# A hybrid Fourier / gated-delta step: the projection stream and its head chains issued in program order, placed by a build-time account of engine times

## The chip, the cores and the metric

The kernel runs on one core of a Trainium2 chip. The metric is the device time of one execution in microseconds (us), median of the runs shown; lower is better. A core has a matrix engine (PE in the profile, which lists its weight loads apart as PEld), a vector engine (DVE), a scalar engine (ACT), a general one (POOL) and a queue that only issues DMAs (SP). Each engine works through its own queue in order; between engines, semaphores say when an operand is ready.

## The reference

One layer with 128 context and 512 latent tokens of width 2048. After an RMS norm and a modulation, one input projection (2048 to 7216 columns) gives a Fourier group, twelve heads of q, k, v and a gate z, and per head and direction a decay and a beta. The heads run a gated delta rule in chunks:

```python
a = lmat + eye
t_inv = triangular_solve(a, eye, left_side=True, lower=True)
...
def step(s, inp):
    u_i, w_i, a_i, qg_i, kd_i, gl_i = inp
    v_new = u_i - einsum(w_i, s)
    o_i = einsum(qg_i, s) + einsum(a_i, v_new)
    s = s * exp(gl_i) + einsum(kd_i, v_new)
    return s, o_i
```

It is run forwards and backwards over the tokens, and the two results are added, normalised and multiplied with silu(z). The Fourier group is a 2D or 3D transform per channel group. All is joined (2048), goes through one output projection, and is added to the input with a gate; a last RMS norm follows. Outputs are both token streams and the final context states of all heads.

## The kernel before

Everything is float32. The three large products are split in two parts (hi and lo, float32r) and computed as three products; the small ones stay float32, which PE runs as two passes (two records in the trace).

**Start.** x is transposed and normalised, the modulation is computed from w_mod, and the first tiles of the projection (k, v, q of head 0, the decays, u of three Fourier groups) are computed while it goes on.

**The projection stream** (`stream`, L1015). Fifty tiles of 128 columns follow, in the order k1 q1 v1 z0 u3, then k, v, q of head h and z of head h-1, and at last f0 to f3 and z11. A tile is two halves of 320 tokens with 48 matmuls each, 4800 in all. Its weights come in on ACT's DMA queue (`raw`, two buffers) and are split by ACT (`whi`, L136) and POOL (`wlo`, L137), five buffers each. Three PSUM banks (`mbank`) take the tiles, five (`bank`) everything else.

**The chains beside it** are Python generators:

- a convolution with SiLU for each k, v, q tile (`conv`, L540 to L554), and the gate z (`after_z`), written to DRAM;
- `solve(h)`: transposes of k, the Gram product (L624), then the inverse of the 32 x 32 triangular blocks on DVE, a series of multiply (L670) and reduce (L672) pairs on 40 partitions; it goes out to DRAM and back twice (`NP`, `DD`);
- `delta(h)`: first the preparation, that is transposes of v, the decays E (L726), the block products that make the full inverse T (L740, L753, L768, L775) and the sums of q squared (`jq`, L786); then the scan, five steps for both directions at once. A step is KT x S (L805), r on DVE (L808), QT x S (L812), T x r (L823), vn on ACT (L826), kd x vn (L831), S on DVE (L839), AT x vn (L844) and the update of o on DVE. It ends with the normalisation of o;
- `head_out(h)`: transposes of o, times z, to DRAM; `fourier(f)`; and `res_gates`, which computes the gates of the residual.

A k or q tile of head i may be evacuated only when `delta(i - 2)` is done (`needs`), since KT and QT have two buffers.

**The output projection** (`out_stream`, L1208) takes the results back from DRAM (`load_y`) in the order heads 0 to 10, Fourier 0 to 3, head 11, in four column passes, 960 matmuls.

What sets the order: the main loop at the file's end runs the stream step by step and resumes each generator when a written-out latency has passed (`yield 3.00, 0.9` means 3 us of waiting and 0.9 us of PE work). That gives the program order. The framework's scheduler then takes it as a priority only: whenever an instruction of an engine isn't ready in its own reckoning, it takes a later one that is. So a stream matmul of a later tile can be issued ahead of a scan step that was written before it.

Of the kernel before, what the change touches and what calls it, by code (L numbers as in the profile page):

```python
# [69 lines left out]

@with_exitstack
def hybrid_step(ctx: ExitStack, tc: tile.TileContext, x_prompt, x_sample, state_ctx, c, c_ctx,
# [3 lines left out]
    PE, ACT, DVE, POOL, SP = nc.tensor, nc.scalar, nc.vector, nc.gpsimd, nc.sync  # L76
    w_mod, w_in, w_out = w_mod[0], w_in[0], w_out[0]
# [366 lines left out]
    def early_back(i, dst, at):  # L444
        SP.dma_start(out=dst[:, at:at + P], in_=ed[i][:, 0:P])
        SP.dma_start(out=dst[:, at + P + (at > 0):at + NT + (at > 0)], in_=ed[i][:, P:NT])
        n, c = (P, i - 1) if i else (48, 3)
        for m, a, b in ((1, at, at + P), (0, at + P + (at > 0), at + NT + (at > 0))):
            ACT.activation(dst[0:n, a:b], dst[0:n, a:b], AF.Identity, bias=ebias[0:n, c, m:m + 1])
# [12 lines left out]
    g = gp.enter_context(tc.tile_pool(name="gdn", bufs=1))  # L462
    def gates():
        abT = g.tile([P, NT], F32, tag="pj", name="abT", bufs=2)
        early_back(0, abT, 0)
        yield 1.50, 0
        pb = bank()
        for t in range(5):
            PE.matmul(pb[:, 48 * t:48 * t + 48], lhsT=abT[:, P * t:P * (t + 1)], rhs=K("sel_ab"), start=True, stop=True)
        pbv = pb[:, 0:240].rearrange("p (t c) -> p c t", c=48)  # L470
        yield 3.00, 0.3
# [20 lines left out]
        yield 5.00, 0.6  # L492
# [8 lines left out]
        yield 0.00, 0  # L501
        gT = g.tile([24, NT], F32, tag="KT", name="gT", bufs=2)
# [5 lines left out]
        yield 4.50, 1.1  # L508
        SP.dma_start(out=gd, in_=gT)
        gT2 = g.tile([24, 4, 5, 32], F32, tag="QT", name="gT2", bufs=2)  # L510
# [27 lines left out]
    def conv(col, parts, dst):  # L538
        ct = (col - C_Q) // P
# [4 lines left out]
        if isinstance(parts, int):  # L544
            early_back(parts, pj, 1)
# [3 lines left out]
        th = g.tile([P, 641], F32, tag="th", name="th", bufs=1)  # L549
        ACT.mul(dst, pj[:, 0:641], cw[:, ct:ct + 1])  # L550
        DVE.scalar_tensor_tensor(dst, pj[:, 1:642], cw[:, 36 + ct:37 + ct], dst, ALU.mult, ALU.add)
        DVE.scalar_tensor_tensor(dst, pj[:, 2:643], cw[:, 72 + ct:73 + ct], dst, ALU.mult, ALU.add)
        ACT.activation(th, dst, AF.Tanh)
        DVE.scalar_tensor_tensor(dst, th, 1.0, dst, ALU.add, ALU.mult)  # L554

# [11 lines left out]
    def after_k(h, parts):  # L567
        s = st_h[h]
        s["KT"] = g.tile([P, 641], F32, tag="KT", name="KT", bufs=2)
        conv(C_K + P * h, parts, s["KT"])  # L570

    def after_v(h, parts):
        s = st_h[h]
        s["vT"] = g.tile([P, 641], F32, tag="vT", name="vT", bufs=1)
        conv(C_V + P * h, parts, s["vT"])

    def after_q(h, parts):
        s = st_h[h]
        s["QT"] = QT = g.tile([P, 641], F32, tag="QT", name="QT", bufs=2)
        conv(C_Q + P * h, parts, QT)  # L580


    def after_z(k, parts):
        zs = g.tile([P, NT], F32, tag="zs", name="zs", bufs=2)
        for a, b, p in parts:
            ACT.activation(zs[:, a:b], p, AF.Tanh, scale=0.5)
            DVE.scalar_tensor_tensor(zs[:, a:b], zs[:, a:b], 1.0, p, ALU.add, ALU.mult)
        SP.dma_start(out=yd[k], in_=zs)

# [6 lines left out]
    def solve(h):  # L596
# [8 lines left out]
        yield 1.50, 0.6  # L605
# [22 lines left out]
        yield 4.50, 1.1  # L628
# [7 lines left out]
        yield 2.50, 0  # L636
# [4 lines left out]
        yield 3.50, 0  # L641
# [6 lines left out]
        yield 6.00, 0  # L648
# [6 lines left out]
        for i in range(1, 8):  # L655
# [5 lines left out]
            yield 1.20, 0  # L661
# [12 lines left out]
        for q in (0, 16):  # L674
            prod(YB[:, 0:8, 0:8], N2[:, q + 8:q + 16, q:q + 8], X2[:, q:q + 8, q:q + 8])
            prod(X2[:, q + 8:q + 16, q:q + 8], X2[:, q + 8:q + 16, q + 8:q + 16], YB[:, 0:8, 0:8])
            yield 2.00, 0
        for r0 in (0, 8):
            prod(YB[:, r0:r0 + 8, 0:8], N2[:, 16 + r0:24 + r0, 0:16], X2[:, 0:16, 0:8])
            yield 3.00, 0  # L680
        prod(YB[:, 0:16, 8:16], N2[:, 16:32, 8:16], X2[:, 8:16, 8:16])
        yield 3.00, 0
        prod(X2[:, 16:24, 0:16], X2[:, 16:24, 16:24], YB[:, 0:8, :])
        yield 3.00, 0
        for c0 in (0, 8):
            prod(X2[:, 24:32, c0:c0 + 8], X2[:, 24:32, 16:32], YB[:, :, c0:c0 + 8])
            yield 3.00, 0
        xd = dram.tile([40, 32, 32], F32, tag="xd", name="xd", bufs=2)
        SP.dma_start(out=xd, in_=X2)
        for b in range(4):  # L690
            SP.dma_start(out=DD[32 * b:32 * b + 32, 0:2].rearrange("p d t c -> p (d t) c"),
                         in_=xd[10 * b:10 * b + 10].rearrange("u r c -> r u c"))
        yield 6.00, 0
        f2 = "p d t c -> p (d t c)"
        DVE.transpose(DD[:, 2:4].rearrange(f2), DD[:, 0:2].rearrange(f2))
        yield 2.00, 0
# [585 lines left out]
```

## Time and profile before

| | us |
|---|---|
| median of 3 runs | 1534.41 (1528.46 to 1538.11) |
| the profiled execution, its own time | 1528.22 |
| its span, first to last instruction | 1526.2 |
| stream: first and last matmul start | 184.6 and 1266.7 |
| output projection: its first matmul starts | 1269.9 |
| mean granted PE clock | 0.975 of full speed |

In the rows of the profile, `mbank<-h_hi,whi` is an instruction that writes `mbank` and reads `h_hi` and `whi`; L and a number is the kernel's line; x and a number counts records. In the groups the columns are busy time, mean time of one in ns, and the idle time before them with what ended it. In the timeline they are start, length, engine, and in brackets the idle time before, with what ended it. A window's row is the stretch, its length, the busy time of PE, PEld, DVE, ACT and POOL, the granted clock, the share of the DMA engines and GB/s. Half clock shows as 0.5 in single stretches; the number of a window is a mean.

### The profile page before, as it was taken

To read this page: it belongs to the slowest core of one execution; us is meant where nothing else is said; L and a number is where in the kernel's file an instruction comes from. 1 tells how busy PE (TensorE), PEld (TensorE's weight loads), DVE (VectorE), ACT (ScalarE), POOL (GpSimd) and SP (SyncE) were. 2 spreads that over 40 slices of the span, in tenths; PEclk is the share of its full clock that TensorE was granted. 3 is DMA by queue.
4 is the path that set the end of the run, shared out by engine and by line. 5 is a ranking of instruction groups with operands and counts; after the bars stand their busy time and mean duration, and the time that the engine had idled before them with its cause. 6 is when DMAs were issued, how large, how long until landed. Compare 5 with 4: busy or idle time off the path is not lost. (4 is left out here: it accounts for less than half of the span.)

```text
span 1526.2 us, 27377 instructions
## 1 busy us (share of the span) xinstructions
PE 1407.7 (92%) x10548; PEld 1270.9 (83%) x10548; DVE 882.6 (58%) x1594; ACT 635.1 (42%) x1678; POOL 643.5 (42%) x759
## 2 busy tenths in 40 slices
PE   6999989889989998989999898999999999999996
PEld 5676989788878897978999898888988998888885
DVE  4455257586867677394756748394856534422025
ACT  5343375244262543526254353526353244322234
POOL 2223346425252542434364344444363433236575
PEclk9999999899999999999999999999999999999999
DMA  9899434315253544433223223323233336386103
GB/s 309 294 336 318 149 114 124 86 39 148 89 157 104 153 119 121 136 96 84 76 84 82 77 80 89 91 72 85 77 95 96 104 114 193 120 301 193 56 1 138
DMA packets 251664, 198.35 MB, mean 130 GB/s; under 512 B 43465, under 2 KB 221590, under 8 KB 251406
## 3 DMA queue, kind: packets, MB, share of 16 engines
q1 hardware_dynamic: 130926, 124.77, 25.5%
q10 hardware_dynamic: 120608, 71.84, 16.5%
q8 instruction: 83, 1.36, 0.4%
q14 instruction: 47, 0.39, 0.1%
HBM read 172.57 MB, written 23.99 MB: 129 GB/s over the span
## 5 line engine op out<-in xcount | busy, mean ns | idle before, releaser
L137 POOL TENSOR_TENSOR wlo<-raw,whi 128x512 fp32r<-128x512 f32 (+1 forms) x276 | 382.1, 1389 | 583.1 <-ACT whi L136 481.1
L1015 PE MATMUL mbank<-h_hi,whi 128*128 128x320 f32 x1600 | 522.9, 327 | 0.0
L1015 PE MATMUL mbank<-h_hi,wlo 128*128 128x320 f32 x1600 | 506.9, 317 | 4.3 <-POOL wlo L137 4.2
L1015 PE MATMUL mbank<-h_lo,whi 128*128 128x320 f32 x1600 | 506.8, 317 | 0.0
L1015 PEld LDWEIGHTS mbank<-h_hi,whi 128*128 128x128 f32 x1600 | 309.8, 194 | 10.5 <-issue 7.9
L1015 PEld LDWEIGHTS mbank<-h_hi,wlo 128*128 128x128 f32 x1600 | 308.6, 193 | 7.3 <-POOL wlo L137 5.6
L1015 PEld LDWEIGHTS mbank<-h_lo,whi 128*128 128x128 f32 x1600 | 309.8, 194 | 1.9 <-issue 1.6
L136 ACT CAST whi<-raw 128x512 fp32r<-128x512 f32 (+1 forms) x276 | 168.2, 614 | 241.1 <-PE mbank L1015 60.8
L670 DVE TENSOR_TENSOR tmp<-NP,XB 40x1024 f32<-40x1024 f32 (+1 forms) x60 | 109.9, 1832 | 1.3
L670 DVE TENSOR_TENSOR tmp<-XB,YB 40x1024 f32<-40x1024 f32 (+1 forms) x60 | 105.8, 1763 | 1.0
L818 POOL TENSOR_SCALAR kd<-k,edl 128x128 f32<-128x128 f32 x96 | 59.8, 634 | 41.6 <-PE bank L831 41.4
L548 ACT COPY pj<-mbank 128x128 f32<-128x128 f32 (+2 forms) x99 | 30.0, 339 | 87.5 <-PE mbank L1015 68.1
L1208 PE MATMUL mbank<-wlo,y_hi 128*128 128x512 f32 x160 | 62.8, 393 | 2.8 <-POOL wlo L137 2.0
L805 PE MATMUL bank<-S,KT 128*128 128x128 f32 x192 | 36.5, 301 | 30.4 <-DVE S L839 30.4
L1208 PE MATMUL mbank<-whi,y_hi 128*128 128x512 f32 x160 | 63.8, 399 | 0.0
L726 ACT ACTIVATE E<-gb,ngg 128x128 f32<-128x128 f32 x120 | 42.2, 394 | 51.8 <-DVE AT L728 31.6
L1208 PE MATMUL mbank<-whi,y_lo 128*128 128x512 f32 x160 | 62.4, 390 | 0.0
L1208 PE MATMUL bank<-whi,y_lo 128*128 128x512 f32 x160 | 62.3, 389 | 0.0
L1208 PE MATMUL bank<-whi,y_hi 128*128 128x512 f32 x160 | 62.3, 389 | 0.0
L1208 PE MATMUL bank<-wlo,y_hi 128*128 128x512 f32 x160 | 62.2, 389 | 0.0
L672 DVE TENSOR_REDUCE YB<-tmp 40x64 f32<-40x512 f32 (+2 forms) x60 | 59.7, 995 | 1.4
L672 DVE TENSOR_REDUCE XB<-tmp 40x64 f32<-40x512 f32 (+2 forms) x60 | 59.7, 995 | 1.3
(319 smaller groups left out, 2440.8 us busy)
## 6 DMA issues: line engine op xcount, KB each, us to landing
raw<-in_w_in ACTq DMA_DIRECT2D x104, 512.0 KB
wm<-in_w_mod SPq DMA_DIRECT2D x64, 512.0 KB
gw<-in_w_mod SPq DMA_DIRECT2D x32, 512.0 KB
raw<-in_w_out ACTq DMA_DIRECT2D x48, 256.0 KB
gb<-gd SPq DMA_DIRECT2D x12, 640.0 KB
yd<-zs SPq DMA_DIRECT2D x16, 320.0 KB
zl<-yd SPq DMA_DIRECT2D x16, 320.0 KB
yd<-zl SPq DMA_DIRECT2D x16, 320.0 KB
```

What stands on the lines that cost most here:

```text
L136: ACT.copy(whi, raw_part)
L137: sub.tensor_tensor(wlo, raw_part, whi, ALU.subtract)
L548: ACT.copy(pj[:, a:b], ps)
L670: DVE.tensor_tensor(tv, A.unsqueeze(2).broadcast_to(s4), B.rearrange("p j c -> p c j").unsqueeze(1).broadcast_to(s4), ALU.mult)
L672: DVE.tensor_reduce(dst, tv, AX.X, ALU.add)
L726: ACT.activation(E[:, 1 - d], gb[:, d, P * t:P * (t + 1)], AF.Exp, bias=ngg4[:, d, h, t:t + 1])
L805: PE.matmul(pks[:, P * d:P * (d + 1)], lhsT=KT[:, a:a + P], rhs=S[:, d], start=True, stop=True)
L818: POOL.tensor_scalar(kd[:, d], k[:, tt[d], :], edl4[:, d, h, tt[d]:tt[d] + 1], 1.0, ALU.mult, ALU.mult)
L1015: PE.matmul(pm[:, 0:320], lhsT=w, rhs=h[k][:, a:b], start=n == 0, stop=n == 3 * NK - 1)
L1208: PE.matmul(acc[t], lhsT=a[kk][:, sl], rhs=w, start=kk == order[0] and j == 0, stop=kk == order[-1] and j == 2)
```

## The change

The latencies at the `yield`s go. In their place stands `Estimate`, called for every instruction as it is built. It keeps a time for each engine and each tile, prices an instruction by its engine, shape and operands (a float32r matmul at 13.5 ns + n / 2.4 ns, a two-operand DVE instruction on 40 partitions at 0.15 us + n / 960 x 1.75 us, and so on), and starts it when its engine, its operands and its buffer are free by that account. A generator is resumed when all that it issued last is done by the account and PE's time is past it by `GUARD`, 0.2 us. Where the stream can't go on, PE's time is set forward to the next such point.

Around the whole main loop stands `tc.manual_schedule()`: from the stream on, the framework takes the program order as it is.

Other edits: `delta` is cut into `prep` and `scan`, run by generators of their own, so that the preparation of the next head may go on beside a scan; `conv` and `after_z` become generators; `take` and `room` count the buffers of `pj`, `th` and `zs`; `th` and `v` get a second buffer; `gT` and `gT2` use the slots of `o` and `v`; the loads of `DD` wait until the head before has read it; the Fourier groups wait for `delta` of head 10.

```diff
+class Estimate:
...
+    def __call__(self, inst, *_):
...
+        t = self.free[engine]
+        for x in ins:
+            y = self.of(x.tensor)
+            t = max(t, y[0] + (0.1 if y[1] != engine else 0.0))
...
+            end = t + self.cost(op, engine, inst, outs, ins)
+            self.free[engine] = end
...
+    room = {"pj": 2, "th": 2, "zs": 2}
...
+    def conv(kind, h, parts):
+        yield from take("pj")
...
-    def delta(h):
+    def prep(h):
...
-        s["v"] = v = g.tile([P, 5, P], F32, tag="v", name="v", bufs=1)
+        s["v"] = v = g.tile([P, 5, P], F32, tag="v", name="v", bufs=2)
...
-        yield 2.50, 1.1
-
-        jq = g.tile([P, 641], F32, tag="th", name="jq", bufs=1)
+        yield
+        yield from take("th")
+        jq = g.tile([P, 641], F32, tag="th", name="jq", bufs=2)
...
+    def scan(h):
...
         while h and ("out", h - 1) not in done:
-            yield 5.50, 0
+            yield "poll"
...
-                yield 3.00, 0.9
+                yield
...
-            while not all(x in done or x[1] < 0 for x in needs(kind, i)):
+            while not (all(x in done or x[1] < 0 for x in needs(kind, i)) and room["pj" if kind in "kqv" else "zs"]):
                 yield
...
-            while not {("u", f), ("f", f), "E_last"} <= done:
-                yield 8.00, 0
+            while not {("u", f), ("f", f), "E_last", ("delta", NH - 2)} <= done:
+                yield "poll"
...
+    def advance():
+        moved = True
+        while moved:
+            moved = False
+            for x in list(live):
+                while x in live and (x[2] is None or x[2] + GUARD <= est.free["PE"]):
+                    poll = x[2] is None
+                    resume(x)
+                    if poll and x[2] is None:
+                        break
+                    moved = True
...
+    ordered = tc.manual_schedule()
+    ordered.__enter__()
...
     while running or live:
+        t = est.free["PE"]
         if running:
             running = next(main, "end") != "end"
-            clock += 0.82
         else:
             next(tail)
-            clock += 3.25
...
+        if est.free["PE"] == t:
+            waits = [x[2] for x in live if x[2] is not None]
+            est.free["PE"] = max(t + 0.05, min(waits) + GUARD if waits else t + 0.5)
+        advance()
```

The lines of the changed kernel are about 150 further down: the stream is L1163, KT x S L948, r L951, QT x S L955, T x r L966, vn L969, kd x vn L974, S L982, AT x vn L987, the solve's pairs L804 and L806, the output projection L1384.

What the change moves shows in the queues. PE's queue in the second and third step of the scan of head 0, before (`h_hi` and `h_lo` are the parts of the stream's input, `whi` and `wlo` of its weights; the numbers are those of buffers):

```order
L831 MATMUL bank_3357<-vn_3322,kd_3318 128x128 x2
L844 MATMUL bank_3363<-vn_3322,AT_2799 128x128 x2
L1015 MATMUL mbank_3508<-h_hi_406,wlo_3297 128x320
L805 MATMUL bank_3372<-S_3360,KT_2079 128x128
L812 MATMUL bank_3373<-S_3360,QT_2109 128x128
L1015 MATMUL mbank_3508<-h_hi_407,whi_3314 128x320
L1015 MATMUL mbank_3508<-h_lo_423,whi_3314 128x320
L1015 MATMUL mbank_3508<-h_hi_407,wlo_3315 128x320
L823 MATMUL bank_3386<-r_3374,KK_2396 128x128 x2
L1015 MATMUL mbank_3508<-h_hi_408,whi_3314 128x320
```

The same place in PE's queue now:

```order
L974 MATMUL bank_3363<-vn_3358,kd_3354 128x128 x2
L987 MATMUL bank_3369<-vn_3358,AT_2802 128x128 x2
L948 MATMUL bank_3378<-S_3366,KT_2119 128x128 x2
L955 MATMUL bank_3379<-S_3366,QT_2221 128x128 x2
L966 MATMUL bank_3396<-r_3380,KK_2495 128x128 x2
L974 MATMUL bank_3402<-vn_3397,kd_3393 128x128 x2
L987 MATMUL bank_3408<-vn_3397,AT_2802 128x128 x2
L948 MATMUL bank_3415<-S_3405,KT_2119 128x128 x2
```

The stream's matmuls have left the scan; heads 1 to 9 read the same, where before 24 of them stood between the steps of most heads, and the next stream matmul of the changed queue comes after the scan. DVE's queue in the scan of head 4, before (`tmp`, `NP`, `XB` and `YB` belong to the solve of head 5):

```order
L839 SCALAR_TENSOR_TENSOR S_7290<-S_7086,egl_2052,bank_7287 128x128 x2
L854 TENSOR_TENSOR o_7085<-o_7085,bank_7293 128x128 x2
L672 TENSOR_REDUCE YB_7207<-tmp_7028 40x8x8
L670 TENSOR_TENSOR tmp_7028<-NP_6949,XB_2064 40x1024
L808 SCALAR_TENSOR_TENSOR r_7329<-bank_7327,neg_eg_2050,v_6544 128x128 x2
L672 TENSOR_REDUCE YB_7207<-tmp_7028 40x16x8
```

And in the scan of head 4 now:

```order
L928 TENSOR_SCALAR q2_7370<-bank_7364 128x5
L804 TENSOR_TENSOR tmp_7332<-NP_7204,XB_2064 40x512
L806 TENSOR_REDUCE YB_7359<-tmp_7332 40x8x8
L804 TENSOR_TENSOR tmp_7332<-XB_2064,YB_7359 40x512
L806 TENSOR_REDUCE XB_2064<-tmp_7332 40x8x8
L804 TENSOR_TENSOR tmp_7332<-NP_7204,XB_2064 40x1024
```

The pairs of the solve stand among the scan's instructions in both; now they start right behind the reading of jq's sums, and three of them stand ahead of the first update of o. At the end of the program, PE's queue at the block products of head 11 before (`T` is built in `KK`; `dft`, `uT` and `V` belong to Fourier group 0):

```order
L1015 MATMUL mbank_13645<-h_hi_408,wlo_13567 128x320
L768 MATMUL bank_13717<-TA_2062,KK_12397 64x64 x10
L1015 MATMUL mbank_13645<-h_hi_409,whi_13566 128x320
L1015 MATMUL mbank_13645<-h_lo_425,whi_13566 128x320
L1015 MATMUL mbank_13645<-h_hi_409,wlo_13567 128x320
L1015 MATMUL mbank_13645<-h_hi_410,whi_13566 128x320
```

And now:

```order
L858 MATMUL bank_13959<-QT_12645,KT_12269 128x128 x2
L876 MATMUL bank_13972<-DD_2060,KK_12486 32x32 x20
L1074 MATMUL bank_14023<-dft_14002,uT_14006 128x256
L1074 MATMUL bank_14023<-dft_14002,V_14009 128x256
L889 MATMUL bank_14027<-DD_2060,YT_2061 32x32 x20
L1074 MATMUL bank_14054<-dft_14002,V_14009 128x256 x2
L905 MATMUL bank_14058<-TA_2062,KK_12486 64x64 x10
```

The block products of head 11 have moved behind the stream's last matmul and behind 120 matmuls of the output projection, next to the Fourier groups.

More of the change, by code (lines that the diff above doesn't have):

```diff
@@ L462, in hybrid_step, with take @@
     g = gp.enter_context(tc.tile_pool(name="gdn", bufs=1))
+    room = {"pj": 2, "th": 2, "zs": 2}
+    def take(tag):
+        while not room[tag]:
+            yield "poll"
+        room[tag] -= 1
     def gates():
+        room["pj"] -= 1
         abT = g.tile([P, NT], F32, tag="pj", name="abT", bufs=2)
-        early_back(0, abT, 0)
-        yield 1.50, 0
+        early_load(0, abT, 0)
+        yield
+        early_bias(0, abT, 0)
+        yield
         pb = bank()
@@ L565, in to_tokens @@
             yield slice(ts[0], ts[0] + n), pb[:, 0:P * n].rearrange("p (t d) -> p t d", t=n), n
[L567 to L580, printed above, removed]
     def after_z(k, parts):
+        yield from take("zs")
         zs = g.tile([P, NT], F32, tag="zs", name="zs", bufs=2)
@@ L1044, in hybrid_step, with resume, begin @@
         after_u(f, u_res[f])
-    after_k(0, 1)
-    after_v(0, 2)
-    after_q(0, 3)
-    done = {("k", 0), ("v", 0), ("q", 0), ("u", 0), ("u", 1), ("u", 2)}
+    done = {("u", 0), ("u", 1), ("u", 2)}
+    live = []
+    def resume(x):
+        est.last = 0.0
+        try:
+            said = next(x[1])
+        except StopIteration:
+            live.remove(x)
+            return
+        if said == "poll":
+            x[2] = None
+        else:
+            x[2] = est.last if said is None else max(est.written(a) for a in said)
+    def begin(rank, steps):
+        x = [rank, steps, 0.0]
+        live.append(x)
+        live.sort(key=lambda y: y[0])
+        resume(x)
[6 more added lines that the diff above has]
+                    poll = x[2] is None
+                    resume(x)
+                    if poll and x[2] is None:
+                        break
+                    moved = True
     fconst = []
@@ L1054, in solves, with preps, scans @@
         for h in range(NH):
-            if ("k", h) not in done:
-                while ("k", h) not in done:
-                    yield 3.50, 0
-                yield 7.00, 0
+            while ("k", h) not in done:
+                yield "poll"
             yield from solve(h)
             done.add(("solve", h))
-    def deltas():
+    def preps():
         for h in range(NH):
             while not {("v", h), ("q", h), ("solve", h)} <= done:
-                yield 2.00, 0
-            yield from delta(h)
+                yield "poll"
+            yield from prep(h)
+            done.add(("prep", h))
+    def scans():
+        for h in range(NH):
+            while ("prep", h) not in done:
+                yield "poll"
+            yield from scan(h)
             done.add(("delta", h))
@@ L1230, in out_stream @@
                     out_norm(t, True)
+    ordered = tc.manual_schedule()
+    ordered.__enter__()
     main, tail = stream(), out_stream()
-    live = [[x(), 0.0] for x in (outs, deltas, solves, fouriers, res_gates)]
-    clock, running = 0.0, True
+    for rank, steps in enumerate((outs, scans, preps, solves, fouriers, res_gates)):
+        begin(2 * rank, steps())
+    for i, kind in enumerate("kvq"):
+        begin(1, conv(kind, 0, i + 1))
+    running = True
     while running or live:
+        t = est.free["PE"]
         if running:
             running = next(main, "end") != "end"
-            clock += 0.82
         else:
             next(tail)
-            clock += 3.25
-        for x in list(live):
-            while x[1] <= clock:
-                try:
-                    lat, busy = next(x[0])
-                except StopIteration:
-                    live.remove(x)
-                    break
-                x[1] = clock + busy + lat
-                clock += busy
-        assert clock < 3000
+        if est.free["PE"] == t:
+            waits = [x[2] for x in live if x[2] is not None]
+            est.free["PE"] = max(t + 0.05, min(waits) + GUARD if waits else t + 0.5)
+        advance()
+        assert est.free["PE"] < 4000
     while next(tail) != "opened":
```

251 lines of the change are left out of this document (187 added, 64 removed).

## The prediction

> **What bounds the kernel now.** I read the page's busy shares first, then the windows of busy time by stage, then who TensorE (PE) waits for, then the timeline of one wait and of one scan, and last the groups of instructions of VectorE (DVE).
>
> ```profile
> span 1526.2 us, 27377 instructions
> ...
> PE 1407.7 (92%) x10548; PEld 1270.9 (83%) x10548; DVE 882.6 (58%) x1594; ACT 635.1 (42%) x1678; POOL 643.5 (42%) x759
> ```
>
> PE is busy for all but 118.5 us. The windows say where those lie; their columns are the stretch, its length, and the busy time of each engine in it. I cut at stream matmul 0 (184.6), 576 (297.7), 4032 (1113.2) and at the end of the stream (1270).
>
> ```profile
> 0.00:184.60 184.60, 165.70 (x1331) 126.42 (x1332) 86.84 (x178) 76.31 (x178) 47.36 (x62) 0.99 0.87 284
> 184.60:297.70 113.10, 98.89 (x734) 95.78 (x732) 70.63 (x103) 58.58 (x152) 58.10 (x78) 0.95 0.41 115
> 297.70:1113.20 815.50, 750.11 (x6115) 700.31 (x6113) 562.79 (x990) 348.32 (x1001) 349.33 (x447) 0.97 0.34 98
> 1113.20:1270.00 156.80, 150.72 (x1245) 147.28 (x1243) 82.12 (x170) 66.10 (x176) 66.54 (x74) 0.98 0.36 108
> 1270.00:1526.20 256.20, 242.27 (x1133) 201.14 (x1131) 80.17 (x155) 85.77 (x173) 122.21 (x100) 0.99 0.42 141
> ```
>
> In the nine periods of the third row PE idles 815.5 - 750.1 = 65.4 us, 7.3 a head, while DVE is at 69% and the others below 45%. So the stream is bound by PE: all that another order can win there is those 65 us and the time lost to a granted clock of 0.97. What it can lose is larger, and the views of PE's waits show why (columns: us in total, times, longest).
>
> ```profile
> PE bank L805 <- DVE S L839: 30.4, 19, 4.5
> PE bank L823 <- DVE r L808: 9.7, 7, 2.8
> ...
> PE bank L831 <- ACT vn L826: 3.3, 6, 0.6
> ```
>
> PE waits above all for DVE inside the scan: the product with the state (L805) for the state update S, the product with T (L823) for r. One such wait in the timeline, DVE first, then PE:
>
> ```profile
> 752.61 2.38 DVE L670 TENSOR_TENSOR tmp<-NP,XB 40x1024 f32<-40x1024 f32 x1
> 755.02 1.21 DVE L672 TENSOR_REDUCE YB<-tmp 40x64 f32<-40x1024 f32 x1
> ...
> 756.56 0.59 DVE L839 SCALAR_TENSOR_TENSOR S<-S,egl,bank 128x128 f32<-128x128 f32 x2
> ...
> 753.56 0.31 PE L1015 MATMUL mbank<-h_hi,wlo 128*128 128x320 f32 x1
> 756.95 0.75 PE L805 MATMUL bank<-S,KT 128*128 128x128 f32 x4 [3.07 <-DVE S L839]
> ...
> 758.42 0.47 PE L1015 MATMUL mbank<-h_lo,whi 128*128 128x320 f32 x1
> 758.68 0.47 PE L1015 MATMUL mbank<-h_hi,wlo 128*128 128x320 f32 x1
> ```
>
> S stood in DVE's queue behind one multiply-and-reduce pair of the next head's solve (752.61 to 756.16), PE had no stream matmul left ahead of L805, and it stood still for 3.07 us. After it the stream matmuls start 0.26 us apart instead of the usual 0.147: half clock. Elsewhere the scan costs nothing, because 24 stream matmuls (3.5 us) stand between its steps.
>
> **The change, part by part.**
>
> *No instruction is added or removed.* The order lists as many computing instructions and DMAs on each engine in both programs; only places change. So PE's work stays, and the sum is over waits. The second buffers of `th` and `v`, `gT` and `gT2` in other slots, the convolution cut into four steps and the `early_load` split issue the same instructions: nothing, hidden by the stream matmuls around them.
>
> *The scans of heads 0 to 9 lose their cover.* In the order of the changed kernel PE has, from head 0 to head 9, the whole scan in one piece: 22 groups of two matmuls, most of which need an earlier one's result by way of DVE or ACT, and no stream matmul among them. The stream stands behind them, since its next tile k(h+2) may only be evacuated after scan h, and later tiles no longer pass. Behind the waiting PE wait the casts of the weights (ACT), the wlo subtractions (POOL) and the loads of w_in on ACT's queue; their five buffers are full then, so they cost nothing later. How long is a bare scan? Its own PE work first, and a scan of the kernel before that ran with little between:
>
> ```profile
> 302.52 0.38 PE L823 MATMUL bank<-v,KK 128*128 128x128 f32 x2
> ...
> 304.32 0.61 PE L844 MATMUL bank<-vn,AT 128*128 128x128 f32 x4
> 304.77 0.61 PE L805 MATMUL bank<-S,KT 128*128 128x128 f32 x4
> ...
> 320.79 0.74 PE L844 MATMUL bank<-vn,AT 128*128 128x128 f32 x4
> ...
> 307.97 0.61 DVE L839 SCALAR_TENSOR_TENSOR S<-S,egl,bank 128x128 f32<-128x128 f32 x2 [1.90 <-PE bank L831]
> ```
>
> A group of two (four records) takes 304.77 - 304.32 = 0.45 us, so 22 groups take 9.9, with the five of jq about 10.5 us. Head 0 needed 302.5 to 321.5, 19 us, with DVE almost free of solve work: that is the floor. In the changed DVE queue it isn't free. Behind the reading of jq's sums (L928 of the changed kernel), which waits for PE at the scan's start, and ahead of the scan's last r or S stand solve pairs: by the order's count 4, 6, 5, 6, 6, 6, 5, 6, 6 and 5 pairs of 1024 elements for heads 0 to 9 and two more of 512 for heads 1, 4, 5, 7 and 8. None can run before PE reaches the scan, and the scan's r and S can't pass them. Their durations:
>
> ```profile
> L670 DVE TENSOR_TENSOR tmp<-NP,XB 40x1024 f32<-40x1024 f32 x36 | 79.1, 2197 | 0.7
> L670 DVE TENSOR_TENSOR tmp<-XB,YB 40x1024 f32<-40x1024 f32 x36 | 72.3, 2009 | 0.7
> L670 DVE TENSOR_TENSOR tmp<-XB,YB 40x512 f32<-40x512 f32 x24 | 33.5, 1395 | 0.3
> ...
> L808 DVE SCALAR_TENSOR_TENSOR r<-bank,neg_eg,v 128x128 f32<-128x128 f32 x96 | 29.3, 340 | 11.5 <-PE bank L805 11.5
> L672 DVE TENSOR_REDUCE XB<-tmp 40x64 f32<-40x1024 f32 x24 | 29.0, 1209 | 0.6
> ...
> L854 DVE TENSOR_TENSOR o<-o,bank 128x128 f32<-128x128 f32 x96 | 23.4, 277 | 8.3 <-PE bank L844 8.2
> L839 DVE SCALAR_TENSOR_TENSOR S<-S,egl,bank 128x128 f32<-128x128 f32 x72 | 22.0, 336 | 17.6 <-PE bank L831 17.6
> ...
> L672 DVE TENSOR_REDUCE YB<-tmp 40x64 f32<-40x512 f32 x24 | 16.2, 676 | 0.6
> ...
> L867 DVE TENSOR_TENSOR o<-o,m 128x640 f32<-128x640 f32 x12 | 12.1, 1005 | 13.9 <-POOL m L866 13.9
> ...
> L864 ACT ACTIVATE jk<-o 128x128 f32<-128x128 f32 x60 | 18.6, 309 | 17.0 <-DVE o L854 7.9 <-DVE o L858 7.0 <-POOL wlo L137 1.8
> ...
> L866 POOL TENSOR_TENSOR m<-m,cst 128x5 f32<-128x5 f32 x12 | 14.9, 1240 | 21.1 <-DVE m L865 21.1
> ```
>
> Pairs: 55 x (2.10 + 1.21) = 182, 10 x (1.4 + 0.68) = 20, together 202 us. The scan's own DVE work: 12 operations of the kind of r (0.34), 6 of S (0.336), 9 additions (0.277), the last multiply (1.0): 9.6, less 2 for what 29 neighbours overlap (two S take 0.61, not 0.67): 7.6 a scan, 76 in all. Where DVE has nothing of the solve left it waits for PE and ACT: twice 1.9 (the idle of the row at 307.97), 0.8 from the first matmul of jq to L928, and at the end 2.1 for the last square, the power on POOL and their hand-overs, since the stream goes on only after the normalising multiply: 6.7 a scan, 67 in all. Ten scans: 202 + 76 + 67 = 345 us; PE works 105 of them and idles 240, 24 a scan. Bounds: 11 a scan (head 0's 19 us and 2.8, less 10.5) and 32 (each hand-over a pair late as in the timeline above). I take 24, because the queue is fixed and its rows are measured.
>
> *Half clock.* A 3.4 us stretch in which PE worked a quarter of the time (753.56 to 757) was followed by half clock. In a bare scan PE works 30% of the time, so it runs at half clock through it and for about 3.4 us of stream behind it: 1.7 us for these, and 0.4 for each of some six groups that nothing hides, 4.2 a scan, 42 in all. What the kernel before loses at a clock of 0.97 goes: 3% of 815.5 is 24 us, of 156.8 3 us.
>
> [...]
>
> *The places around the scans.* Head 10's scan keeps stream matmuls between its steps. The block products of a head now stand some 20 to 90 stream matmuls (3 to 13 us) apart instead of 24; I keep 8 of the 65 us idle for them in the third row and 3 in the fourth, between none and all. In the second row the same solves and block products lie on PE; of 14.2 us idle I take half away: 105. The end: the block products and scan of head 11 with the four Fourier groups lie among six groups of 15 output matmuls, where head 11's products had stream matmuls before; between nothing and one bare scan (24), I take 10. PE time that moves across 1270 is lost there and found here.
>
> *SP and POOL.* The steps' DMAs move with them (S, DD, zs, gb); SP issues in program order and PE waits of a DMA are not among the three rows above. POOL's kd stands before the matmul that needs it by a whole step. Both at nothing, covered by the scan's DVE queue; without that cover kd's time would show.
>
> **The sum** (us): 184.6 + 105 + (750 - 24 + 9 x 24 + 9 x 4.2 + 8 = 988) + (150.7 - 3 + 24 + 4.2 + 3 = 179) + (256.2 + 10 = 266) = 1723 against the span of 1526.2. The execution's own time was 1528.22, 2 more than its span and 6 under the median of 1534.41: 1725.
>
> **Rivals.** (a) The scans run bare but at head 0's pace, the pairs passing in gaps: 11 idle a scan, 1725 - 130 = 1595. For it: those 19 us were measured; against it: DVE's fixed queue. (b) The other side: the hand-overs are as short as PE's waits for vn, 3.3 us in 6, 0.55 each. Fourteen a scan make 7.7 us idle and no half clock: 1725 - 163 - 42 = 1520, no change. It decides from about 8 us of idle a scan, which is what the waits removed (65 and 14) give back over ten. Against it: even head 0 needed 19 us for 10.5 of PE work. (c) The order rests on estimates, and where an engine is later than estimated PE now waits at every step: six block steps a head at 1.6 us (30.4 / 19) for eleven heads are 105 more, 1830. For it: nothing can pass; against it: the 3 to 13 us between them. (d) No half clock: 1725 - 42 = 1683; against it the wait shown. That the change doesn't do what it says is out: the order shows it.
>
> [...]
>
> **How the numbers follow.** Forecast 0.62; (a) 0.10; (b) 0.04; (c) 0.12; (d) 0.12. The predicted time is the first. The range, 1640 to 1815, holds it with bounds of 17 and 31 idle a scan, (d) and half of (c), and leaves out (a), (b) and the rest. About 1% is what a measurement of this kernel can tell from no change: (b) lies half within it and half below, so faster 0.02, same 0.02, slower 0.96.
>
> **What would show it.** PE idle should rise from 118 to some 330 us, in ten pieces where no stream matmul starts for 30 to 45 us; in them PE waits for DVE S and r, and DVE's rows stand without gaps until the pairs are through. The granted clock should be 0.5 in them. Between two scans 384 stream matmuls should pass with hardly a wait. Wrong: if the pieces last near 20 us, (a); if the clock stays at 1, (d); if the waits lie at the block products, (c).

## The result and the profile after

The changed kernel takes 1841.16 us (median of 3 runs, 1836.22 to 1841.55) against 1534.41: ratio 1.201, 95% interval 1.197 to 1.205. The forecast was 1725, with a range of 1640 to 1815: the sign was right, the size too small by 116 us. The profiled execution has a span of 1839.4 us. Its page, first lines:

```profile
span 1839.4 us, 27427 instructions
...
PE 1509.8 (82%) x10548; PEld 1356.2 (74%) x10548; DVE 888.8 (48%) x1594; ACT 635.3 (35%) x1678; POOL 626.8 (34%) x759
```

PE has as many matmuls as before and is idle for 329.6 us in place of 118.5; that is the total that the forecast gave, though its parts lie elsewhere. But it is also busy for 102 us more with the same work, since the mean granted clock fell from 0.975 to 0.878. The windows of the changed kernel, cut at the start of stream matmuls 0, 575 and 4031 and of the first output matmul (columns as before: stretch, length, busy time of PE, PEld, DVE, ACT and POOL, granted clock, DMA share, GB/s; the kernel before was cut at matmuls 576 and 4032, which lie 0.5 and 1.7 us behind 575 and 4031 there):

```profile
0.00:186.20 186.20, 166.52 (x1332) 126.55 (x1332) 86.99 (x178) 76.34 (x177) 41.92 (x58) 0.98 0.86 278
186.20:342.90 156.70, 101.06 (x692) 99.24 (x690) 71.46 (x118) 56.81 (x145) 48.67 (x66) 0.80 0.27 74
342.90:1330.30 987.40, 811.22 (x6066) 755.68 (x6066) 530.83 (x941) 341.89 (x983) 330.48 (x444) 0.85 0.29 81
1330.30:1519.50 189.20, 157.35 (x1153) 153.08 (x1151) 97.00 (x163) 62.61 (x173) 72.54 (x77) 0.89 0.28 81
1519.50:1839.40 319.90, 273.69 (x1313) 221.69 (x1313) 102.53 (x197) 97.64 (x201) 133.15 (x116) 0.93 0.37 124
```

| stage (us) | before | forecast | after | after - forecast |
|---|---|---|---|---|
| to stream matmul 0 | 184.6 | 184.6 | 186.2 | 2 |
| to matmul 575 | 113 | 105 | 156.7 | 52 |
| nine periods of the stream | 815 | 988 | 987.4 | -1 |
| to the first output matmul | 157 | 179 | 189.2 | 10 |
| output stage | 256 | 266 | 319.9 | 54 |

So the nine periods, the forecast's largest term, came out as written; the start and the end did not. Who PE waits for (us in total, times, longest):

```profile
PE bank L966 <- DVE r L951: 80.9, 28, 8.8
PE mbank L1163 <- ACT whi L254: 43.9, 1, 43.9
PE bank L1021 <- DVE o L1010: 35.9, 8, 5.7
PE bank L1119 <- DMA gw<-in_w_mod: 24.6, 13, 9.9
PE bank L974 <- ACT vn L969: 19.9, 34, 0.6
PE bank L923 <- ACT jq L919: 17.6, 7, 4.9
PE mbank L1384 <- ACT y_hi L1280: 12.7, 1, 12.7
...
PE bank L905 <- DVE TA L892: 3.9, 1, 3.9
...
PE bank L912 <- ACT ET L907: 3.3, 3, 2.0
...
PE bank L876 <- DVE KK L863: 1.1, 2, 0.7
```

Before, S and r of the scan led this list with 30.4 and 9.7 us. Now r leads with 80.9; new are one stop of the stream of 43.9 us, the waits for the normalised o and for the gate weights gw (1.7 and 4.9 us before), and one of 12.7 us where the output begins.

A step of the scan of head 5, in the timeline (start, length, engine; in brackets the idle time before it):

```profile
918.12 1.89 DVE L804 TENSOR_TENSOR tmp<-NP,XB 40x1024 f32<-40x1024 f32 x1
...
918.38 1.06 PE L955 MATMUL bank<-S,QT 128*128 128x128 f32 x4
920.05 1.21 DVE L806 TENSOR_REDUCE YB<-tmp 40x128 f32<-40x1024 f32 x1
921.18 0.59 DVE L951 SCALAR_TENSOR_TENSOR r<-bank,neg_eg,v 128x128 f32<-128x128 f32 x2
...
921.66 0.68 PE L966 MATMUL bank<-r,KK 128*128 128x128 f32 x4 [2.23 <-DVE r L951]
921.70 1.88 DVE L804 TENSOR_TENSOR tmp<-XB,YB 40x1024 f32<-40x1024 f32 x1
...
923.62 1.21 DVE L806 TENSOR_REDUCE XB<-tmp 40x128 f32<-40x1024 f32 x1
...
924.75 0.59 DVE L982 SCALAR_TENSOR_TENSOR S<-S,egl,bank 128x128 f32<-128x128 f32 x2
```

DVE works with hardly a gap here: a pair of the solve, r, a pair, S. PE's T x r (L966) waits for r, which stands behind a pair. Between the last stream matmul ahead of a scan and the first behind it lie, by the starts of the stream matmuls, 41.3 to 46.0 us in ten pieces, 432 in all. Three windows of the same kernel, a part of this scan, its end and the stretch from there to the next piece:

```profile
914.00:930.00 16.00, 9.96 (x44) 8.57 (x44) 15.71 (x21) 2.30 (x9) 0.72 (x2) 0.71 0.00 0
930.00:947.00 17.00, 12.37 (x49) 11.41 (x50) 9.75 (x21) 6.59 (x24) 1.29 (x4) 0.50 0.24 66
947.00:1006.00 59.00, 59.00 (x495) 58.26 (x494) 22.02 (x47) 25.71 (x70) 27.69 (x35) 1.00 0.36 98
```

In the first, DVE is busy for 15.71 of 16 us. The scan's end runs at half clock; after that PE runs 59 us at full clock without any wait.

### The profile page after: what moved, and what is told of

It is laid out like the page before. It is cut to its first block, busy times and chain, and to the rows that moved or that the text cites. A ratio compares the mean times of both kernels' runs of the same rounds, so it can differ in the third digit from the quotient of the medians.

```text
span 1839.4 us, 27427 instructions
## 1 busy us (share of the span) xinstructions
PE 1509.8 (82%) x10548; PEld 1356.2 (74%) x10548; DVE 888.8 (48%) x1594; ACT 635.3 (35%) x1678; POOL 626.8 (34%) x759
## 4 chain that ended last, share of the span: by engine, by line
PE 54%; DVE 18%; DMA 11%; ACT 4%; issue 3%; POOL 2%; SPq 0%; ACTq 0%; DVEq 0%; POOLq 0%
PE mbank L1163 31%; DVE tmp L804 7%; PE bank L1384 4%; PE mbank L1384 3%; DMA gw<-in_w_mod 2%; DMA raw<-in_w_out 2%; PE bank L966 2%; DMA raw<-in_w_in 2%; DVE YB L806 2%; PE bank L974 2%; PE bank L987 2%; DVE XB L806 2%; PE bank L516 2%; DMA yt<-yd 1%; DVE tmp L792 1%
## 5 line engine op out<-in xcount | busy, mean ns | idle before, releaser
L255 POOL TENSOR_TENSOR wlo<-raw,whi 128x512 fp32r<-128x512 f32 (+1 forms) x276 | 371.7, 1360 | 629.2 <-ACT whi L254 533.7
L1163 PE MATMUL mbank<-h_hi,whi 128*128 128x320 f32 x1600 | 512.9, 321 | 43.9 <-ACT whi L254 43.9
L1163 PE MATMUL mbank<-h_hi,wlo 128*128 128x320 f32 x1600 | 500.5, 313 | 3.3 <-POOL wlo L255 3.3
L1163 PE MATMUL mbank<-h_lo,whi 128*128 128x320 f32 x1600 | 500.5, 313 | 0.0
L1163 PEld LDWEIGHTS mbank<-h_hi,whi 128*128 128x128 f32 x1600 | 307.0, 192 | 55.8 <-ACT whi L254 44.1
L1163 PEld LDWEIGHTS mbank<-h_hi,wlo 128*128 128x128 f32 x1600 | 306.0, 191 | 3.8 <-POOL wlo L255 3.8
L1163 PEld LDWEIGHTS mbank<-h_lo,whi 128*128 128x128 f32 x1600 | 306.6, 192 | 0.0
L969 ACT ACTIVATE vn<-bank,s 128x128 f32<-128x128 f32 x120 | 37.5, 363 | 302.0 <-PE bank L966 302.0
L863 DVE TENSOR_TENSOR KK<-KK,E 128x256 f32<-128x256 f32 x60 | 34.5, 576 | 182.8 <-ACT E L862 182.8
L966 PE MATMUL bank<-r,KK 128*128 128x128 f32 x192 | 45.6, 379 | 80.9 <-DVE r L951 80.9
L966 PEld LDWEIGHTS bank<-r,KK 128*128 128x128 f32 x192 | 36.5, 265 | 89.2 <-issue 49.9
L804 DVE TENSOR_TENSOR tmp<-NP,XB 40x1024 f32<-40x1024 f32 (+1 forms) x60 | 99.3, 1655 | 0.9
L804 DVE TENSOR_TENSOR tmp<-XB,YB 40x1024 f32<-40x1024 f32 (+1 forms) x60 | 95.6, 1593 | 1.0
L1009 POOL TENSOR_TENSOR m<-m,cst 128x5 f32<-128x5 f32 x12 | 14.2, 1183 | 207.6 <-DVE m L1008 207.6
L1384 PE MATMUL mbank<-whi,y_hi 128*128 128x512 f32 x160 | 64.6, 404 | 19.5 <-ACT y_hi L1280 12.7
L974 PE MATMUL bank<-vn,kd 128*128 128x128 f32 x192 | 49.8, 403 | 28.0 <-ACT vn L969 19.9
L850 POOL TENSOR_TENSOR gb<-gb,cst 128x640 f32<-128x640 f32 x24 | 33.4, 1412 | 113.3 <-DMA gb<-gd 113.3
L974 PEld LDWEIGHTS bank<-vn,kd 128*128 128x128 f32 x192 | 39.0, 278 | 39.1 <-issue 29.5
L1384 PE MATMUL mbank<-wlo,y_hi 128*128 128x512 f32 x160 | 64.1, 400 | 4.1 <-POOL wlo L255 3.9
L1384 PE MATMUL mbank<-whi,y_lo 128*128 128x512 f32 x160 | 63.6, 397 | 0.0
```

The source lines that it names most:

```text
L255: sub.tensor_tensor(wlo, raw_part, whi, ALU.subtract)
L804: DVE.tensor_tensor(tv, A.unsqueeze(2).broadcast_to(s4), B.rearrange("p j c -> p c j").unsqueeze(1).broadcast_to(s4), ALU.mult)
L966: PE.matmul(pv[:, P * d:P * (d + 1)], lhsT=T[:, 1 - d, tt[d], :], rhs=r[:, d] if step >= 0 else v[:, 0, :], start=True, stop=True)
L969: ACT.mul(vn[:, d], pv[:, P * d:P * (d + 1)], s["s3"][:, d, tt[d]:tt[d] + 1])
L974: PE.matmul(pu[:, P * d:P * (d + 1)], lhsT=kd[:, d], rhs=vn[:, d], start=True, stop=True)
L1163: PE.matmul(pm[:, 0:320], lhsT=w, rhs=h[k][:, a:b], start=n == 0, stop=n == 3 * NK - 1)
```

## The experiments

**The two halves of the change, each alone.** e1 keeps the account's program order and lets the scheduler pass instructions again; e2 is the kernel before with the exact order of its own program.

```diff
-    ordered = tc.manual_schedule()
-    ordered.__enter__()
...
-    ordered.__exit__(None, None, None)
```

> The changed kernel without the manual schedule: the program order still comes from the account, but the framework's scheduler may again issue a later instruction that is ready. In the order 43 to 127 stream matmuls (6 to 19 us) now stand inside the scans of heads 0 to 9, where the changed kernel has none. Theory (the bare scans and the stalls of an exact order each cost their part): about 1700 us, 1640 to 1750. Rival 1 (exact issue alone is the loss): 1530 to 1580. Rival 2 (the places that the account gives are the loss, and issuing has nothing to do with it): over 1790.

```diff
+    ordered = tc.manual_schedule()
+    ordered.__enter__()
     main, tail = stream(), out_stream()
...
+    ordered.__exit__(None, None, None)
```

> The kernel before, with its written-out latencies, but issued in exactly its program order from the stream on. Its scans keep 186 to 198 stream matmuls among their steps (heads 1 to 9). Theory (the loss is that the scans are bare, not that the order is exact): 1545 to 1600 us, some waits of 1 to 3 us per step more than before. Rival (nothing can pass, so every late hand-over stops PE, wherever it is): over 1680 us, waits at the steps of the scan and at the block products.

e1: 1550.69 us, ratio to the kernel before 1.010 (1.006 to 1.014). e2: 1851.29 us, 1.205 (1.201 to 1.209). Both of my first expectations fell and both rivals for "exact issue" held. The account's order by itself costs 16 us. Set free, though, it isn't the changed kernel's queue: the scheduler puts 43 to 127 stream matmuls back into the scans of heads 0 to 9. So e1 alone doesn't part the bare scans from the exact order; e2 does. Exact issue costs the old order, whose scans have nearly 200 stream matmuls among their steps, 317 us, as much as the new one. PE's waits in e2 (L823 is T x r there, L805 KT x S, L740 the first block product and L768 a later one, L563 the transposes):

```profile
PE bank L740 <- DVE KK L727: 79.8, 22, 39.7
PE bank L823 <- DVE r L808: 51.4, 18, 4.8
PE bank L805 <- DVE S L839: 28.8, 17, 3.3
PE bank L563 <- DVE KT L554: 19.7, 8, 3.9
PE bank L768 <- DVE TA L756: 19.4, 9, 5.6
```

Apart from two at the start, of 39.7 and 7.1 us, none of them is longer than 5.6 us, and they lie at every kind of step, in the scans and outside. So covering the scan in the queue doesn't save an exact order: what is late still stops PE.

**One engine's order exact, the others free**, all with the account's program order:

```diff
-    ordered = tc.manual_schedule()
+    ordered = tc.manual_schedule(engines={mybir.EngineType.PE})
```

> The changed kernel's program order, exact on PE alone; the scheduler orders DVE, ACT, POOL and SP. PE's queue is the changed kernel's: no stream matmul in the scans of heads 0 to 9. Theory A (PE's own order is the loss: what PE meets late, it waits for): 1760 to 1850 us. Theory B (DVE's order is the loss: r and S behind the solve's pairs): with DVE free the scans run at head 0's pace of 22 us instead of 43, about 1841 - 10 x 20 = 1640 us. Theory C (the orders of ACT, POOL and SP hold weights and decays back): under 1620.

> The same program order, exact on DVE alone. PE may be filled: 103 to 208 stream matmuls stand in the scans of heads 1 to 9. Theory A (PE's order): under 1600 us, as free as before. Theory B (DVE's order): 1700 to 1800, since r and S stand behind the same pairs, though the stream hides part. Theory C (ACT, POOL, SP): under 1600.

> The same program order, exact on every engine but DVE, which the scheduler orders. Theory A (PE's order): 1760 to 1850 us, as the changed kernel. Theory B (DVE's order): about 1640, the waits of PE for r and S gone. Theory C (ACT, POOL, SP): 1760 to 1850.

> The same program order, exact on every engine but PE, which the scheduler orders; 17 to 48 stream matmuls (2.5 to 7 us) stand in the scans of heads 1 to 9. Theory A (PE's order): under 1650 us. Theory B (DVE's order) and theory C (ACT, POOL, SP): 1841 less what the matmuls in the scans cover, 9 x 3 to 7 us, so 1770 to 1820.

> The changed kernel's program order, exact on ACT alone; in the order 16 to 48 stream matmuls stand in the scans of heads 0 to 9. Theory D (ACT's order holds the stream: the copies that empty the PSUM of tile k(h+2) and the casts of the weights stand behind the scan's vn, so a free PE has at most one half tile, 48 matmuls, to fill a scan with): 1760 to 1830 us, nearly all of the loss. Rival (POOL's or SP's order does it): under 1600.

> The same program order, exact on SP alone (DMA issues); 88 to 231 stream matmuls stand in the scans. Theory D (ACT's order): 1540 to 1570 us, as the free kernel. Rival (loads behind stores that wait for DVE, the queue of SP): over 1700.

> The same program order, exact on POOL alone; 57 to 97 stream matmuls stand in the scans. Theory D (ACT's order): 1540 to 1580 us. Rival (wlo of the weights behind the sums on gb and the powers that wait for DVE, the queue of POOL): over 1700.

> The changed kernel's program order, exact on PE and ACT; the scheduler orders DVE, POOL and SP. Theory (the orders of PE and ACT carry the loss): 1800 to 1840 us. Rival (each exact engine adds its own part: PE 184 and ACT 172 over the free kernel's 1551 overlap, and DVE, POOL and SP add the rest): 1735 to 1780.

> The same program order, exact on DVE, POOL and SP; the scheduler orders PE and ACT; 74 to 98 stream matmuls stand in the scans. Theory (PE and ACT carry the loss; POOL's 57 us and SP's 38 overlap): 1590 to 1650 us. Rival (any three exact orders lock each other): over 1720.

| exact on | us | over none (1550.69) |
|---|---|---|
| DVE (e6) | 1542.76 | -8 |
| SP (e10) | 1588.23 | 38 |
| POOL (e11) | 1607.19 | 57 |
| ACT (e9) | 1722.37 | 172 |
| PE (e5) | 1734.20 | 184 |
| DVE, POOL, SP (e15) | 1720.82 | 170 |
| PE, ACT (e14) | 1769.76 | 219 |
| all but DVE (e7) | 1823.21 | 273 |
| all but PE (e8) | 1828.45 | 278 |
| all | 1841.16 | 290 |

These are single runs, except none and all. Runs of the kernel before, taken beside them, lay between 1528.1 and 1542.8 us, so a difference of 10 us between two rows tells nothing. No theory held throughout: e5 and e9 lie between theirs, e8 lies 8 us above its highest range, e10 and e11 lie 18 and 27 us above theory D and far below its rival, e14 and e15 where their rivals put them. DVE's order alone costs nothing, so theory B fell, though it is in DVE's queue that r stands behind the pairs. PE's or ACT's order alone brings more than half of the loss; the five single engines add up to 443 us where all together cost 290, while DVE, POOL and SP cost 170 together and 87 singly. And freeing one engine of five gives back 18 (DVE) or 13 us (PE), little more than such runs differ by. A loss of this kind isn't a sum over engines. The likely reason, that one engine that may pass still waits for those that may not, was not tested by itself.

How ACT's order alone can hold PE shows in one copy, the one that empties the PSUM banks of tile k7 (stream matmuls 2400 to 2495). ACT's timeline with DVE alone exact (e6), where the scan of head 5 lasts from 769.7 to 811.7 us; the copy comes in two halves, and a third row belongs to the first half of the next tile:

```profile
759.74 0.49 ACT L683 COPY pj<-mbank 128x128 f32<-128x128 f32 x2 [0.65 <-PE mbank L1163]
...
768.23 0.43 ACT L683 COPY pj<-mbank 128x320 f32<-128x320 f32 x1 [1.81 <-POOL wlo L255]
...
773.46 0.62 ACT L996 ACTIVATE o<-bank,eg 128x128 f32<-128x128 f32 x2 [0.63 <-PE bank L955]
779.19 0.49 ACT L683 COPY pj<-mbank 128x128 f32<-128x128 f32 x2 [5.10 <-PE mbank L1163]
```

And in the changed kernel, whose scan of head 5 ends at 937:

```profile
935.75 0.62 ACT L969 ACTIVATE vn<-bank,s 128x128 f32<-128x128 f32 x2 [5.14 <-PE bank L966]
...
940.00 0.79 ACT L683 COPY pj<-mbank 128x128 f32<-128x128 f32 x3
```

The copy needs nothing of the scan, but it is written behind it. Free, each half comes within 1 us of its last matmul, ahead of the scan, and the next tile's first half is copied in the scan, among whose steps 194 stream matmuls stand. Exact, it comes behind the last vn, 44 us after the tile's last matmul (it starts at 895.4), and with two of the three PSUM banks of the stream held no more than a half tile, 48 matmuls, stands in a scan of heads 0 to 9 (e8, e9). In e9 PE also waits for such copies themselves:

```profile
PE mbank L1163 <- ACT pj L683: 20.0, 6, 6.4
```

This mechanism was read from the orders and the traces; no run took this copy alone.

**The solve's pairs.** The order of e4 is the changed kernel's on every engine, since the account charges the pairs as before.

```diff
         def prod(dst, A, B):
             ni, nj, ncol = A.shape[1], A.shape[2], B.shape[2]
...
+            A, B, dst, ni, ncol, nj = A[:, 0:1, 0:1], B[:, 0:1, 0:1], dst[:, 0:1, 0:1], 1, 1, 1
...
```

> The changed kernel with each engine's order the same, but the 16 multiply-and-reduce instructions of 512 and 1024 elements in a head's solve work on one element, so the inverse is left out but for its diagonal blocks. Theory (these instructions in DVE's queue set the length of a bare scan): the pieces without a stream matmul shrink from 43 to about 30 us, the waits of T x r for r from 80.9 to under 20 us in all, the stop at 267 us by some 22 us, 1841 - 130 - 22 = 1690 us, 1650 to 1720. Rival (hand-overs and the half clock set that length): the pieces stay over 38 us, 1780 to 1820 us.

1696.0 us; PE's waits:

```profile
PE mbank L1168 <- ACT whi L254: 20.6, 1, 20.6
...
PE bank L971 <- DVE r L956: 10.7, 17, 1.7
```

The ten pieces shrink from 432 to 303 us, the waits for r from 80.9 to 10.7, the stop of the stream from 43.9 to 20.6. As expected, then: where nothing may pass, the pairs in DVE's queue lengthen a bare scan, by 13 of its 43 us. The other 30 stay without them.

**Half clock.** e13 puts matmuls that nobody reads on PE while it waits in the scans:

```diff
+    def fill(ps, h, n):
...
+        for _ in range(n if h < 10 else 0):
+            PE.matmul(ps[:, 256:512], lhsT=hi_t[0][:, 0:128], rhs=hi_t[1][:, 0:256], start=True, stop=True)
...
+                fill(pqs, h, 18)
```

> The changed kernel in the same order, with idle matmuls (f32r, 128x256, their result is read by nobody) put on PE in steps 1 to 4 of the scans of heads 0 to 9: 18 behind QT x S, 5 behind T x r, 5 behind AT x vn, some 3.4 us a step at full clock. They keep PE at work while it waits. Theory (a bare scan is as long as DVE's queue; half clock mostly hides behind it): the half clock inside the pieces falls from 25 us each to under 8, the pieces shorten by 2 to 6 us, total 1780 to 1825 us. Rival 1 (half clock sets the length): under 1760. Rival 2 (half clock costs nothing, or the idle matmuls stand in the way): 1835 to 1880.

1866.78 us. The window of the nine periods (cut at its stream matmuls 575 and 4031):

```profile
342.30:1352.50 1010.20, 888.57 (x7075) 839.65 (x7074) 534.07 (x942) 343.95 (x984) 330.98 (x442) 0.93 0.29 79
```

Its clock rises from 0.85 to 0.93, so its half clock falls from some 296 to some 141 us (twice the missing share of each window); yet the pieces grow from 432 to 457. Rival 2 held: half clock doesn't set the length of a bare scan, or no more than these idle matmuls cost by standing in the way. Which of the two isn't settled.

**The start.** The stop of the stream at 267 us, from the queues of SP, POOL and ACT in the changed kernel's timeline:

```profile
288.90 0.28 SPq L823 DMA_DIRECT2D xd<-XB  x1
...
294.99 0.42 SPq L847 DMA_DIRECT2D gb<-gd  x1
...
300.01 2.59 POOL L850 TENSOR_TENSOR gb<-gb,cst 128x640 f32<-128x640 f32 x2 [47.17 <-DMA gb<-gd]
...
302.72 0.83 ACT L685 ACTIVATE vT<-pj,cw 128x641 f32<-128x641 f32 x1 [48.56 <-POOL pj L676]
...
310.48 0.62 ACT L254 CAST whi<-raw 128x512 fp32r<-128x512 f32 x1 [0.84 <-DMA raw<-in_w_in]
```

The load of gb stands in SP's queue behind the store of head 0's solve, which DVE finishes at 288.9; POOL's sums wait for gb, the zeroes of pj stand behind them, ACT's vT behind those, the weights' cast behind vT, and the stream behind the cast.

```diff
-        SP.dma_start(out=gb, in_=gd2[h].partition_broadcast(P))
...
+        ACT.dma_start(out=gb, in_=gd2[h].partition_broadcast(P))
```

> The changed kernel, each engine's order word for word the same, but the load of gb (the decays of a head) is issued from ACT's queue and not from SP's, where it stands behind the store of the solve's result. Theory (that queue stops the stream for 43.9 us at 267 us: gb, then POOL's sums, then the zeroes of pj, then vT on ACT, then whi): the stall goes, 1841 - 40 = 1800 us, 1790 to 1810. Rival (the stall only moves to the next wait, that for the inverted blocks DD): 1830 to 1845 us.

> The same program order, exact on all engines but DVE, and gb loaded from ACT's queue. Theory (the stop at 267 us has two causes, each enough by itself: gb in SP's queue behind the solve's store, and the instructions on sk in DVE's queue behind the solve): the stop of 36 to 44 us is gone, matmul 575 comes 35 to 45 us earlier than with either alone, total 1780 to 1795 us against 1823 with DVE free alone. Rival (a third wait takes its place): over 1810.

e3: 1841.4 us, nothing gained; vT moves 43 us forward, and ACT now waits further down its queue for DVE's work on sk of head 1, which stands behind head 0's pairs:

```profile
298.93 0.63 ACT L761 ACTIVATE KK<-bank,ns 128x128 f32<-128x128 f32 x2 [36.60 <-DVE ns L751]
```

e18 frees DVE as well: 1817.1 us, 6 below e7, which is no difference between single runs. A third wait takes the place of the two, ACT's for gr, between 200 and 330 us:

```profile
ACT gr L769 <- DVE gr L768: 34.0, 1, 34.0
```

The rival held both times: PE's stop is 43.9 us in the changed kernel, 36.2 in e3 and 32.6 in e18. It has at least three causes, each nearly enough: the solve of head 0 is long, and everything that is written behind any part of it waits.

**The end, and versions that might beat both.** A GUARD of -4 us writes the steps earlier: of all heads and in a free order in e12, of the last two heads in e16 (all engines exact) and e17 (DVE alone exact).

```diff
-                while x in live and (x[2] is None or x[2] + GUARD <= est.free["PE"]):
+                while x in live and (x[2] is None or x[2] + (GUARD if ("delta", 9) not in done else -4.0) <= est.free["PE"]):
```

> The changed kernel without the manual schedule and with GUARD at -4 us in place of 0.2: a step is written into the program 4 us of the account's PE time earlier, and the scheduler takes that as a priority. 39 to 110 stream matmuls stand in each scan, and head 11's scan lies at stream matmul 4661 and not behind 120 output matmuls. Theory (the account's order loses at the end, where head 11 and the Fourier groups come late, and nowhere else once the order is not exact): 1505 to 1530 us, below the kernel before. Rival (the order inside the stream is no better than before): 1535 to 1560.

> The changed kernel, exact on every engine, with a GUARD of -4 us once head 9 is done (0.2 before): the steps of the last two heads are written earlier, head 11's scan lies at stream matmul 4554 with 84 stream matmuls in it, and not behind 120 output matmuls. Theory (the end is long because head 11's products and scan lie bare in the first output pass): that pass takes about 95 us instead of 128, part of it given back in the stream, total 1790 to 1825 us. Rival (the end is long by loads and weights that come late, wherever head 11 stands): 1835 us or more.

> The changed kernel's program order, exact on DVE alone, with the GUARD of -4 us once head 9 is done; head 11's scan lies at stream matmul 4578. With DVE alone exact the stream ended at 1248 us, 19 earlier than in the kernel before, and the first output pass took 111 us against 79. Theory (only head 11's late place stood between that order and a gain): 1505 to 1525 us, under the kernel before. Rival (what the end gains the stream loses): 1530 to 1550.

e12: 1551.23 us, 1.012 (1.007 to 1.017). e17: 1576.8 us, 1.029 (1.026 to 1.032): none beats the kernel before. e12's rival held. e17 lies above both of its ranges and 34 us above e6, the same without the earlier steps: its first output pass is 47 us shorter than e6's, its stream ends 75 us later. e16: 1843.63 us, as the changed kernel. Its windows from stream matmul 4031 to the first output matmul, and of the first output pass:

```profile
1331.40:1603.00 271.60, 209.42 (x1506) 194.29 (x1504) 133.55 (x288) 84.01 (x232) 77.32 (x95) 0.86 0.26 77
1603.00:1659.20 56.20, 56.20 (x239) 46.20 (x240) 21.53 (x17) 20.65 (x34) 21.01 (x16) 0.96 0.70 214
```

With head 11 and the Fourier groups in the stream the pass takes 56 us, not 128, and has no idle time, so late loads don't set its length, as the rival had it; but the stretch ahead of it takes 272 and not 189, so the theory's total fell as well. What the end gains the stream loses.

## Why the prediction was wrong in size

**"The stream is bound by PE"; "no instruction is added or removed."** Both held: 10548 matmuls, and e1, the same program order set free, needs 1.0% more than before.

**"The scans of heads 0 to 9 lose their cover."** As a picture of this kernel it held: ten pieces of 41 to 46 us (forecast: 30 to 45), DVE busy for 34 of the 43 us, r late, and e4 shows the pairs behind 13 us of each. As the whole cause it didn't: it put the loss in the place where the scan stands in PE's queue, and e2, which has the cover there, loses as much. What e1, e2 and the runs by engine show is wider: no queue may pass a late instruction. PE's or ACT's queue alone is enough for more than half of the loss, and so are DVE's, POOL's and SP's together.

**"I take 24", and half clock 4.2 a scan.** Their sum held, their split didn't, so that an agreement within 1 us is partly luck. The nine periods have 987.4 - 811.2 = 176 us idle, where the terms give 9 x 24 + 8 = 224, and 811 us busy where they give 750 - 24 + 38 = 764. In the mean of the ten pieces PE is busy for 25.0 us and idle for 18.2, not 10.5 and 24: the scan's own matmuls ran at half clock inside the waits (290 of the 432 us of the pieces were at half clock), so part of what I counted as idle was slow work. In the kernel before, the half clock behind the wait of 3.07 us lasted from 757.79 to 761.20, 3.4 us as taken; PE was busy for 0.84 of the 3.42 us ahead of it, and for 0.37 of the 3.44 us from 753.56 to 757, not a quarter of them. A period came out as a piece of 43 us and 67 us of stream, where the terms give 37 (10.5 + 24 + 6 x 0.4) and 73 (988 / 9 less that). The pieces are longer in part because more pairs ran in them than the 65 counted: their rows there add up to 237 us, not 202. The transposes of o and the products of `res_gates` wait in some pieces too, but the two pieces without either last 41.7 and 42.4 us.

**"SP and POOL: both at nothing."** This step failed, and with it "of 14.2 us idle I take half away: 105": 156.7 us. The forecast found no DMA in the three rows of PE's waits that it shows and took the moved loads as covered. The same view has one, in just this stretch:

```profile
PE bank L740 <- DMA DD<-xd: 7.6, 1, 7.6
```

It is the wait for the result of head 0's solve, back from DRAM, and half of the 14.2 us. The load of gb reaches PE in the changed kernel only by way of two other queues: it ran late through SP, POOL and ACT to the stream, 43.9 of the 52 us. That it has several sufficient causes (e3, e18) makes it a matter of the fixed queues, not of one DMA.

**"The end: ... between nothing and one bare scan (24), I take 10."** This step failed as well, in its size: 54 us in the output stage and most of the 10 ahead of it. The first pass took 128 us against 79. e1 needs 99 there, so 20 go with the place that the account gave head 11, and 29 with the exact order. Of the 20, 12 are PE work of head 11 and the Fourier groups that stood in the stream before; the forecast had left it there. The later passes took 180 us against 167 (e1: 168), 12 for the exact order. Ahead of the pass stands the wait of 12.7 us for y_hi. The bound of one bare scan left out that each of head 11's products and the Fourier groups would stand bare as well.

**The rivals.** (a) and (b) fell: r waits behind its pairs. (c) came nearest in time, 1830, and its reason, that nothing can pass, is the one that e1 and e2 bear out; but its waits were others: the block products wait for some 8 us in all (L905, L912, L876), the start and the end for the rest. (d) fell: a mean clock of 0.878 over 1839 us is 448 us of half clock (before: 76), although e13 leaves open what it costs. The window just ahead of the half clock from 930 to 947 above:

```profile
926.70:930.10 3.40, 1.00 (x7) 0.65 (x6) 3.37 (x5) 0.12 (x1) 0.00 (x0) 1.00 0.00 0
```

The clock was full and PE busy for 1.00 of the 3.40 us, 29%; its longest wait in the 13 us ahead of 930 was 2.23 us (one of 3.5 us, ending at 942.5, lies inside the half clock). So half clock came here behind waits of at most 2.23 us with matmuls between them.

**The range.** It held the unknown of the scans, which came out on the forecast, and nearly nothing for the start and the end (a few us each), where the error lay.

## What to carry to other kernels

An order that every engine must keep is a bet on every estimate at once: try it with one engine fixed at a time, and with the old order fixed, before working on the order itself. A forecast for such an order has to follow each queue at the program's start and end too, where nothing covers a late load: one DMA in a shared queue can stop an engine three queues away. When a stop has several sufficient causes, taking one away gains nothing; that doesn't show that it was harmless.

## What the runs showed of the hardware

Half clock went with PE busy for 73% of a stretch of the changed kernel by its records (12.37 of 17.00 us at 0.50), not only with an idle PE; at half clock the records themselves are longer (0.47 us for a stream matmul of the kernel before, 0.31 at full clock). It began behind 3.40 us with PE busy for 29% of them (1.00 us), in the kernel before behind 3.42 us with 25% (0.84 us). Cut into steps of 3.41 us, the shortest stretch in the clock's records, the traces of the kernel before and the changed one have 43 steps at full clock with PE busy for under 40%, and each was followed by half clock; none of the 732 with 70% or more was. Matmuls that only keep PE at work raised the clock of the nine periods from 0.85 to 0.93 and shortened nothing (987.4 us without them, 1010.2 with them).
